# End of layer 0: joining tile 0 by TensorE ahead of a branch, and splitting a weight chunk on ScalarE and VectorE in place of GpSimd

## The chip, the cores and the metric

The kernel runs on one core of one Trainium2 chip. The metric is the device time of one execution in microseconds (us). TensorE is called PE, VectorE DVE, ScalarE ACT, GpSimd POOL and SyncE SP, as in the profile.

## The reference, cut to what matters

A model of two layers works on 256 latent and 256 context tokens of 1024 features. Each layer is a mixer (layer 0: convolution and neighbourhood attention; layer 1: windowed attention), a residual with a layer norm, a mixture of 16 experts of which each token uses two, and a second residual with a layer norm. What matters here is the seam between the layers:

```python
h_lat = layer_norm(alpha * h_lat + m_lat[5] * y[:, y.shape[1] - n_lat:], ln_g[i, 1], ln_b[i, 1])
if need_ctx:
    h_ctx = layer_norm(alpha * h_ctx + m_ctx[5] * y[:, :n_ctx], ln_g[i, 1], ln_b[i, 1])
...
u_lat = h_lat * (1.0 + m_lat[1]) + m_lat[0]
u_ctx = h_ctx * (1.0 + m_ctx[1]) + m_ctx[0]
...
q_lat, k_lat, v_lat = jnp.split(u_lat @ w_in, [q_cols, q_cols + kv_cols], axis=-1)
k_ctx, v_ctx = jnp.split(u_ctx @ w_in[:, q_cols:], [kv_cols], axis=-1)
```

`y` holds for each token the sum of its two experts' rows, each times the token's weight. The layer norm of that sum, turned to feature-major form and scaled, is the input of layer 1's first projections (v, then k, then q).

## The kernel before, in words

The 512 tokens are four tiles of 128 rows, `nt(0)` to `nt(3)` (the SBUF tiles N). In `moe` the experts' work runs in 11 units; each unit's rows are multiplied by the modulation and scattered to a DRAM tensor `yd` with two slots per token. The last two units (`TAIL0 = 2`) are not scattered: their rows stay in SBUF (`self.last`, the tiles wh), and `comb(t, i, p)` brings the rows of unit i to tile t by two TensorE products with a matrix of weights, one for each half of 512 features, into a pair of PSUM banks p.

What the other units gave comes from DRAM: `join_load` reads for tile t both slots, 1024 features each, into one 128x2048 buffer (`zs[t]`; tiles 0 and 1 are named wl, tiles 2 and 3 x). `join_first(t)` adds slot 0 times the token's weight to N, by one DVE instruction (tile 0, L1986) or by two of POOL, a multiplication in place and an addition (tiles 1 to 3, L1983 and L1984). `join_second(t)` adds slot 1 times its weight by one DVE instruction (L1999).

At the end of the last unit's second `down` half come, in the code's order: `comb(0, 0)` into the pair `self.first`; `overflow`, a branch on a number read from SBUF, which every engine reads and takes by itself and which skips a long body where no expert has too many tokens (L1588, L1589); `join_first(0)` on DVE and `join_first(1)` on POOL; and the multiplication of the last rows (L1510).

Then `run` loads the square root's table and lets ACT round the first weight chunk of layer 1 (w1 chunk 5, the v columns) to its high part (L2432). `u1` follows: `comb(0, 1)`, the combinations of tiles 1 and 2, then for tile t: `sums(t)` adds the PSUM pair to N and takes statistics (DVE, L2037, L2038, and a chain of small instructions with a square root on ACT), `norm(t)` normalises on ACT (L2046), `half(t, h)` transposes four blocks by PE (L567), scales them on ACT (L2058; the last on DVE, L2056), rounds them to the high part H (ACT L2064 for tiles 0 and 1, POOL L2062 for 2 and 3) and takes the low part L on DVE (L2066). Tile t's v products (L411 to L413, in `inproj1`) need H and L of both halves. `split1` computes the first chunk's low part on POOL (L2435). The second chunk (the k columns) is split on POOL in two instructions over 2048 columns, high (L388) and low (L391), behind the joins of tiles 2 and 3; its buffer then goes back to the weight stream, and SP issues the next load (L323). The k projection, the first group of the loop in `inproj1`, uses this split chunk.

Every engine takes its instructions in the order of the code; the plan of `moe` (`plan0`) sets the order up to the last unit, and `u1` is written out by hand.

Of the kernel before, what the change touches and what calls it, by code (L numbers as in the profile page):

```python
# [11 lines left out]
F32 = mybir.dt.float32  # L12
# [4 lines left out]
OP = mybir.AluOpType  # L17
# [41 lines left out]
TAIL0 = 2  # L59
# [212 lines left out]
class Kern:  # L272
# [1152 lines left out]
    def moe(self, td, rt, m5base, m5rows, consts):  # L1425

        nc, W, V = self.nc, self.W, self.nc.vector
# [61 lines left out]
        def down(u, f):  # L1489
            w, give = chunks(dw, u, 2)  # L1490
            p = self.mm()
            self.down(p, hT[u], w, f)
            if f:
                give()
            yield
            if u == N - 1:

                end.append(p)
                if f == 0:
                    yield  # L1500
                    return
                self.first = [self.mm() for h in range(2)]
                for i in range(TAIL0 - 1):
                    self.comb(0, i, self.first)
                self.overflow(4, S, td, rt, m5rows)
                self.join_first(0, rt["wt"], False)
                self.join_first(1, rt["wt"], True)
            for f, p in enumerate(end) if u == N - 1 else ((f, p),):
                s = slice(f * 512, f * 512 + 512)
                V.tensor_tensor(ys[u][:, s], p, ys[u][:, s], op=OP.mult)  # L1510
            yield
# [5 lines left out]
        def turn(u):  # L1517
# [9 lines left out]
                                        op0=OP.is_equal, op1=OP.mult)  # L1527
            if u == N - 2:
                self.affine1()
            if u == N - 1:  # L1530
                for k in range(1, 3):
                    self.after[self.end0 - k] = i.ins.name
                self.limit = self.end0
                self.pump()
# [453 lines left out]
    def comb(self, t, i, p):  # L1988

        y, c, _ = list(self.last.values())[i]  # L1990
        for h in range(2):
            self.nc.tensor.matmul(p[h], c[:, t * 128:t * 128 + 128], y[:, h * 512:h * 512 + 512], start=(i == 0),
                                  stop=(i == TAIL0 - 1), skip_group_check=True)
        return p

    def join_second(self, t, wt):

        n, (z, held) = self.nt(t), self.zs.pop(t)
        self.nc.vector.scalar_tensor_tensor(n, z[:, 1024:2048], wt[:, 1, t:t + 1], n, op0=OP.mult, op1=OP.add)  # L1999
        self.release(held)  # L2000


# [23 lines left out]
    def u1(self, wt):  # L2026
# [41 lines left out]

        def comb(t, p):
            ps[t] = p  # L2070
            for i in range(TAIL0):
                self.comb(t, i, p)

        ps = {0: self.comb(0, TAIL0 - 1, self.first)}
        comb(1, [self.mm(), self.mm()])
        comb(2, [self.pv(), self.aux()])
        self.join_second(0, wt)
        norm(0, sums(0))
        self.join_second(1, wt)
        self.split1()  # L2080
        for t in range(2, 4):
            self.join_first(t, wt, True)
        self.wq.append(self.split(pool=True))
        lo = []
        for t in range(4):
            a, b = half(t, 0), half(t, 1)
            next(a)
            if t < 3:
                rs = sums(t + 1)
            next(a)  # L2090
            if t < 3:
                norm(t + 1, rs)
            if t:
                next(lo.pop())
            if t < 2:
                self.join_second(t + 2, wt)
            next(b)
            next(b)
            if t == 0:
                comb(3, [self.mm(), self.mm()])  # L2100
            next(a)
            lo.append(b)
            if t == 3:
                next(b)
            if t:
                yield t - 1
        for *_, held in self.last.values():
# [488 lines left out]
```

## Time and profile before

| what | us |
|---|---|
| median of 3 runs | 795.43 |
| lowest and highest of them | 790.47 and 797.7 |
| the profiled execution | 796.22 |
| its span in the trace | 794.4 |

The trace is of one execution, the profiled one, and its times count from the span's start; 1.8 us of that execution lie around the span. TensorE is busy for 706.9 us (89%), VectorE 470.4 (59%), ScalarE 278.2 (35%), GpSimd 231.4 (29%). A TensorE product of 128x512 in f32 stands as two records in the trace. The timeline view merges like instructions that follow each other (xN), and its start is the time at which the instruction was taken up, so a wait inside the instruction shows as a longer duration.

### The profile page before, as it was taken

Reading aid. Unit: us, or ns where it says so; the run is one execution under the profiler, and the core shown is the slowest. Engines: PE = TensorE matmul, PEld = TensorE weight load, DVE = VectorE, ACT = ScalarE, POOL = GpSimd, SP = SyncE. Lnnn points to the kernel's source line nnn. Section 1 sums busy time; section 2 is a strip of 40 time slices with the busy share of each in tenths; the row PEclk is TensorE's granted clock in tenths of the full one; section 3 lists DMA queues with packets and bytes.
Section 4 is the critical chain, followed back from the end, with each engine's and each line's share of the span. In section 5 each row is a group of like instructions: output and inputs, shape, how many; then the busy total and the mean of one; then the engine's idle time right before and its main releaser. Section 6 shows DMA issues by size and latency. Waiting matters only on the chain. (4 is left out here: it accounts for less than half of the span.)

```text
span 794.4 us, 11446 instructions
## 1 busy us (share of the span) xinstructions
PE 706.9 (89%) x4162; PEld 414.5 (52%) x4162; DVE 470.4 (59%) x1000; ACT 278.2 (35%) x611; POOL 231.4 (29%) x250
## 2 busy tenths in 40 slices
PE   4799999979989987999999787979999986999992
PEld 0477676724567764434433337856556763454430
DVE  0589897747754878622334298397676388532115
ACT  0541212036775254101100145545677533211121
POOL 1200000037631002854000192163377460111111
PEclk9799999979999997999999997999999997999997
DMA  9974665557459368999997931637645493998892
GB/s 360 388 284 170 239 238 201 224 204 265 142 179 336 120 222 305 376 353 350 413 413 314 386 144 54 212 132 277 282 165 188 179 346 138 412 421 320 349 370 86
DMA packets 36252, 209.64 MB, mean 264 GB/s; under 512 B 4439, under 2 KB 4695, under 8 KB 15056
## 3 DMA queue, kind: packets, MB, share of 16 engines
q1 hardware_dynamic: 27888, 183.56, 59.8%
q10 hardware_dynamic: 4816, 13.85, 5.4%
q0 software_dynamic: 3472, 11.31, 4.0%
q8 instruction: 36, 0.59, 0.3%
q14 instruction: 40, 0.33, 0.1%
HBM read 197.92 MB, written 12.06 MB: 264 GB/s over the span
## 5 line engine op out<-in xcount | busy, mean ns | idle before, releaser
L631 DVE SCALAR_TENSOR_TENSOR x<-x,sm,x 128x512 f32<-128x512 f32 x120 | 90.7, 756 | 3.4
L411 PE MATMUL mm<-H,wh 128*128 128x512 f32 (+1 forms) x208 | 78.5, 378 | 2.4 <-ACT H L614 2.4
L412 PE MATMUL mm<-L,wh 128*128 128x512 f32 (+1 forms) x208 | 76.1, 366 | 0.0
L413 PE MATMUL mm<-H,wl 128*128 128x512 f32 (+1 forms) x208 | 75.9, 365 | 0.2 <-DVE wl L391 0.2
L480 PE MATMUL aux<-w,sc 128*32 128x512 f32 x368 | 53.8, 679 | 17.0 <-ACT sc L444 7.6
L391 DVE TENSOR_TENSOR wl<-w,wh 128x512 fp32r<-128x512 f32 (+1 forms) x27 | 39.1, 1486 | 21.2 <-ACT wh L390 21.0
L401 POOL TENSOR_SCALAR wh<-w 128x256 fp32r<-128x256 f32 x32 | 13.3, 417 | 118.0 <-DMA w<-wo 118.0
L411 PEld LDWEIGHTS mm<-H,wh 128*128 128x128 f32 x208 | 40.2, 193 | 14.3 <-issue 3.4
L699 DVE TENSOR_REDUCE mx<-mm 128x1 f32<-128x512 f32 (+1 forms) x64 | 39.3, 615 | 13.5 <-PE mm L786 7.4
L1838 POOL TENSOR_TENSOR yl<-ada,yh 128x512 fp32r<-128x512 f32 x12 | 15.3, 1274 | 102.3 <-ACT yh L1835 102.3
L412 PEld LDWEIGHTS mm<-L,wh 128*128 128x128 f32 x208 | 40.1, 193 | 7.3 <-DVE L L617 0.8
L413 PEld LDWEIGHTS mm<-H,wl 128*128 128x128 f32 x208 | 40.0, 192 | 7.3 <-DVE wl L391 0.8
L723 ACT COPY pT<-tp 128x512 f32<-128x512 f32 (+1 forms) x64 | 33.9, 530 | 25.2 <-PE tp L721 24.9
L411 PE MATMUL mm<-wh,H 128*128 128x512 f32 x104 | 42.4, 408 | 0.0
L412 PE MATMUL mm<-wl,H 128*128 128x512 f32 x104 | 40.7, 391 | 0.0
L1404 PE MATMUL aux<-x,H 128*32 128x512 f32 (+2 forms) x104 | 38.4, 609 | 0.0
L1510 DVE TENSOR_TENSOR y<-mm,y 128x512 f32<-128x512 f32 x18 | 12.3, 690 | 41.8 <-PE mm L1422 41.7
L390 ACT CAST wh<-w 128x512 fp32r<-128x512 f32 (+1 forms) x27 | 29.6, 1139 | 7.0 <-PE mm L413 6.9
L714 POOL TENSOR_SCALAR pexp<-pexp,ss 128x512 f32<-128x512 f32 x32 | 22.4, 700 | 31.7 <-DVE ss L713 23.8
L413 PE MATMUL mm<-wh,L 128*128 128x512 f32 x80 | 31.4, 393 | 0.0
L714 POOL TENSOR_SCALAR x<-x,ss 128x256 f32<-128x256 f32 (+1 forms) x32 | 21.1, 660 | 32.5 <-DVE ss L713 23.1
L1404 PE MATMUL pv<-w,X 128*32 128x512 f32 (+2 forms) x96 | 30.1, 596 | 0.0
(471 smaller groups left out, 1691.6 us busy)
## 6 DMA issues: line engine op xcount, KB each, us to landing
w<-ada_w SPq DMA_DIRECT2D x46, 1024.0 KB, 6.8
x<-exp SPq DMA_DIRECT2D x35, 1024.0 KB, 13.6
w<-exp SPq DMA_DIRECT2D x32, 1024.0 KB, 6.6
w<-w SPq DMA_DIRECT2D x15, 1024.0 KB, 10.4
wh<-exp SPq DMA_DIRECT2D x12, 1024.0 KB, 10.3
wl<-exp SPq DMA_DIRECT2D x12, 1024.0 KB, 9.6
w<-wo SPq DMA_DIRECT2D x8, 1024.0 KB, 9.8
yd<-x ACTq DMA_DIRECT2D x1, 4096.0 KB, 16.8
```

Source lines behind the costliest of these rows:

```text
L390: self.nc.scalar.copy(h[:, s], w[:, s])
L391: (self.nc.gpsimd if pool or low else self.nc.vector).tensor_tensor(l[:, s], w[:, s], h[:, s].bitcast(F32), op=OP.subtract)
L411: t.matmul(out, ah, bh, start=start, stop=False, skip_group_check=onto)
L412: t.matmul(out, ah, bl, start=False, stop=False, skip_group_check=onto)
L413: t.matmul(out, al, bh, start=False, stop=stop, skip_group_check=onto)
L480: nc.tensor.matmul(p[32 * j:32 * j + 32, :], self.sc[:, kt, :], w[:, j * 512:(j + 1) * 512], start=(kt == 0), stop=(kt == 7), skip_group_c ...
L631: nc.vector.scalar_tensor_tensor(acc[:, i], src, w, acc[:, i], op0=OP.mult, op1=OP.add)
L699: nc.vector.reduce_max(mx, p[:, :nk], axis=AX.X, negate=True)
L714: nc.gpsimd.tensor_scalar(P[i][:, :nk], P[i][:, :nk], r[:, 0:1], 0.0, op0=OP.mult, op1=OP.add)
L723: nc.scalar.copy(T[i][:, :nk], t[:, :nk])
L1404: self.nc.tensor.matmul(p[r], x(kt)[:, r], w_j[:, kt % 4 * 512:kt % 4 * 512 + 512], start=(kt == 0), stop=(kt == 7), skip_group_check=True)
L1838: (V if u == N - 1 else nc.gpsimd).tensor_tensor(lo, y, hi.bitcast(F32), op=OP.subtract)
```

## The change

Tile 0 is joined by PE: `join(0)` adds both slots to the PSUM pair `self.first` by four products with diagonal matrices (identity times the tokens' weight), ahead of `comb(0, 0)` and of the branch. The two diagonals are built by two DVE instructions in the `turn` of the last unit but one. `join_first(0)` and `join_second(0)` on DVE go. Tile 1's second slot is joined by two products with a third diagonal (tile `pexp`, one DVE instruction at the start of `u1`), and `join_second(1)`'s instruction goes. Tile 1's first slot stays on POOL, and tiles 2 and 3 stay as they were.

The combination of tile 2 is moved behind the transposes of tile 0, and that of tile 3 behind those of tile 1. The second weight chunk's high part is one ACT instruction over 2048 columns behind `norm(0)`, its low part four DVE instructions over 512 columns each: two in the turn of tile 2, two in that of tile 3. The two POOL instructions go. The chunk's buffer is given back after the last of the four.

```diff
                 self.first = [self.mm() for h in range(2)]
+                self.join(0, self.first)
                 for i in range(TAIL0 - 1):
                     self.comb(0, i, self.first)
                 self.overflow(4, S, td, rt, m5rows)
-                self.join_first(0, rt["wt"], False)
                 self.join_first(1, rt["wt"], True)
...
             if u == N - 2:
                 self.affine1()
+                self.joins = {}
+                self.join_weights(W.tile([128, 2, 128], F32, name="diag"), ((0, 0), (0, 1)), rt["wt"])
...
+    def join_weights(self, d, which, wt):
+
+        for i, (t, k) in enumerate(which):
+            self.nc.vector.tensor_scalar(d[:, i], self.ident, wt[:, k, t:t + 1], None, op0=OP.mult)
+            self.joins.setdefault(t, []).append((k, d[:, i]))
+
+    def join(self, t, p):
+
+        for i, (k, x) in enumerate(self.joins[t]):
+            for h in range(2):
+                o = k * 1024 + h * 512
+                self.nc.tensor.matmul(p[h], x, self.zs[t][0][:, o:o + 512], start=(i == 0), stop=False, skip_group_check=True)
...
         ps = {0: self.comb(0, TAIL0 - 1, self.first)}
+        self.join_weights(W.tile([128, 4, 128], F32, name="pexp", bufs=5), ((1, 1),), wt)
         comb(1, [self.mm(), self.mm()])
-        comb(2, [self.pv(), self.aux()])
         self.join_second(0, wt)
         norm(0, sums(0))
-        self.join_second(1, wt)
+        w, whole = self.take(), self.held
+        wlo, whi = self.part("wh"), self.part("wl")
+        nc.scalar.copy(whi, w)
         self.split1()
         for t in range(2, 4):
             self.join_first(t, wt, True)
-        self.wq.append(self.split(pool=True))
+        self.wq.append((whi, wlo))
...
-            if t < 2:
-                self.join_second(t + 2, wt)
             next(b)
             next(b)
             if t == 0:
+                comb(2, [self.pv(), self.aux()])
+                self.join_second(1, wt)
+            if t == 1:
                 comb(3, [self.mm(), self.mm()])
+            if t < 2:
+                self.join_second(t + 2, wt)
             next(a)
             lo.append(b)
             if t == 3:
                 next(b)
+            if t > 1:
+                for i in (2 * t - 4, 2 * t - 3):
+                    q = slice(i * 512, i * 512 + 512)
+                    nc.vector.tensor_tensor(wlo[:, q], w[:, q], whi[:, q].bitcast(F32), op=OP.subtract)
+                if t == 3:
+                    self.release(whole)
```

`join_second` keeps only the giving back of the buffer for a tile that is in `self.joins`, and `comb` starts a PSUM pair only where no join has started it.

VectorE behind the branch, before: N is the residual's tile, the wl tiles are the loaded slots, the wh tile of L1510 is the last unit's rows, mm the PSUM pair.

```order
L1986 SCALAR_TENSOR_TENSOR N_1818<-wl_3483,rwt,N_1818 128x1024
L1510 TENSOR_TENSOR wh_3438<-mm,wh_3438 128x512 x2
L1999 SCALAR_TENSOR_TENSOR N_1818<-wl_3483,rwt,N_1818 128x1024
L2037 TENSOR_TENSOR N_1818<-N_1818,mm 128x512
L2038 BN_STATS bst<-N_1818 128x6
```

VectorE at the same place, now:

```order
L1510 TENSOR_TENSOR wh_3441<-mm,wh_3441 128x512 x2
L2001 TENSOR_SCALAR pexp<-cb,rwt 128x128
L2053 TENSOR_TENSOR N_1818<-N_1818,mm 128x512
L2054 BN_STATS bst<-N_1818 128x6
L2053 TENSOR_TENSOR N_1818<-N_1818,mm 128x512
L2054 BN_STATS bst<-N_1818 128x6
```

Both joins of tile 0 are gone from VectorE, and one diagonal has come in.

GpSimd behind the branch, before: the second tile wl and the tiles x are the loaded slots, w of L2435 is the first chunk's low part, wh and the wl of L391 the second chunk's parts, H the high part of the transposed tiles.

```order
L1983 TENSOR_SCALAR wl_3487<-wl_3487,rwt 128x1024
L1984 TENSOR_TENSOR N_1818<-N_1818,wl_3487 128x1024
L2435 TENSOR_TENSOR w_6110<-x_3490,x_6109 128x2048
L1983 TENSOR_SCALAR x_3492<-x_3492,rwt 128x1024
L1984 TENSOR_TENSOR N_1819<-N_1819,x_3492 128x1024
L1983 TENSOR_SCALAR x_3495<-x_3495,rwt 128x1024
L1984 TENSOR_TENSOR N_1819<-N_1819,x_3495 128x1024
L388 TENSOR_SCALAR wh_6162<-w_3498 128x2048
L391 TENSOR_TENSOR wl_6163<-w_3498,wh_6162 128x2048
L2062 TENSOR_SCALAR H_6120<-pT 128x4x128
```

GpSimd at the same place, now:

```order
L2464 TENSOR_TENSOR w_6116<-x_3493,x_6115 128x2048
L1985 TENSOR_SCALAR x_3495<-x_3495,rwt 128x1024
L1986 TENSOR_TENSOR N_1819<-N_1819,x_3495 128x1024
L1985 TENSOR_SCALAR x_3498<-x_3498,rwt 128x1024
L1986 TENSOR_TENSOR N_1819<-N_1819,x_3498 128x1024
L2078 TENSOR_SCALAR H_6126<-pT 128x4x128
```

The two instructions over the second chunk are gone, and the rounding of tile 2 follows the joins directly.

TensorE from the branch to the transposes of tile 1, before: the wh tiles are the rows of the last two units, cb holds the identity, mm, pv and aux are PSUM banks.

```order
L1992 MATMUL mm<-wh_3438 128x512 x2
L1992 MATMUL mm<-wh_3348 128x512 x2
L1992 MATMUL mm<-wh_3438 128x512 x2
L1992 MATMUL pv<-wh_3348 128x512
L1992 MATMUL aux<-wh_3348 128x512
L1992 MATMUL pv<-wh_3438 128x512
L1992 MATMUL aux<-wh_3438 128x512
L567 MATMUL tp<-cb,N_1818 128x128 x8
```

TensorE at the same place, now:

```order
L1994 MATMUL mm<-wh_3441 128x512 x2
L2009 MATMUL mm<-wl_3490,pexp 128x512 x2
L1994 MATMUL mm<-wh_3348 128x512 x2
L1994 MATMUL mm<-wh_3441 128x512 x2
L567 MATMUL tp<-cb,N_1818 128x128 x8
L1994 MATMUL pv<-wh_3348 128x512
L1994 MATMUL aux<-wh_3348 128x512
L1994 MATMUL pv<-wh_3441 128x512
L1994 MATMUL aux<-wh_3441 128x512
```

Two products for tile 1's second slot have come in, and the combination of tile 2 stands behind the transposes of tile 0.

## Rows read from the trace of the kernel before

**Rows 1.** The page: the span.

```profile
span 794.4 us, 11446 instructions
```

**Rows 2.** The table by stretch, late layer 1: us, busy per engine, PEclk, DMA share, GB/s.

```profile
680.00:700.00 20.00, 19.95 (x99) 11.00 (x100) 10.54 (x21) 3.66 (x9) 2.55 (x2) 1.00 1.01 422
```

**Rows 3.** Timeline of DVE, 453 to 493: start, duration, line, operation, idle before and releaser.

```profile
453.20 3.29 DVE L1986 SCALAR_TENSOR_TENSOR N<-wl,rwt,N 128x1024 f32<-128x1024 f32 x1 [4.83 <-DVEq L1589]
456.42 1.27 DVE L1510 TENSOR_TENSOR wh<-mm,wh 128x512 f32<-128x512 f32 x2
457.62 5.58 DVE L1999 SCALAR_TENSOR_TENSOR N<-wl,rwt,N 128x1024 f32<-128x1024 f32 x1
463.30 0.69 DVE L2037 TENSOR_TENSOR N<-N,mm 128x512 f32<-128x512 f32 x1
...
474.28 5.00 DVE L2066 TENSOR_TENSOR L<-pT,H 128x512 fp32r<-128x512 f32 x1
479.20 0.67 DVE L2037 TENSOR_TENSOR N<-N,pv 128x512 f32<-128x512 f32 x1
...
492.58 0.69 DVE L2066 TENSOR_TENSOR L<-pT,H 128x512 fp32r<-128x512 f32 x1 [2.15 <-POOL H L2062]
```

**Rows 4.** Timeline of POOL, 448 to 479.

```profile
448.51 1.12 POOL L1983 TENSOR_SCALAR wl<-wl,rwt 128x1024 f32<-128x1024 f32 x1 [13.73 <-DMA wl<-yd]
453.07 2.34 POOL L1984 TENSOR_TENSOR N<-N,wl 128x1024 f32<-128x1024 f32 x1 [3.44 <-DVEq L1589]
457.62 4.50 POOL L2435 TENSOR_TENSOR w<-x,x 128x2048 fp32r<-128x2048 f32 x1 [2.21 <-ACT x L2432]
462.10 2.08 POOL L1983 TENSOR_SCALAR x<-x,rwt 128x1024 f32<-128x1024 f32 x1
...
466.59 1.12 POOL L1983 TENSOR_SCALAR x<-x,rwt 128x1024 f32<-128x1024 f32 x1
467.80 3.20 POOL L1984 TENSOR_TENSOR N<-N,x 128x1024 f32<-128x1024 f32 x1
...
473.37 5.36 POOL L391 TENSOR_TENSOR wl<-w,wh 128x2048 fp32r<-128x2048 f32 x1
```

**Rows 5.** Timeline of ACT: the first chunk's rounding and the first norm.

```profile
455.66 1.88 ACT L2432 CAST x<-x 128x2048 fp32r<-128x2048 f32 x1
...
467.19 1.24 ACT L2046 ACTIVATE N<-N,brs 128x1024 f32<-128x1024 f32 x1 [0.48 <-DVE brs L550]
```

**Rows 6.** Timeline of PE: combinations, and first and last of the k projection.

```profile
451.77 1.98 PE L1992 MATMUL mm<-wh 128*128 128x512 f32 x4
457.15 6.81 PE L1992 MATMUL mm<-wh 128*128 128x512 f32 x12 [3.39 <-DVE wh L1510]
...
497.84 0.39 PE L411 MATMUL mm<-H,wh 128*128 128x512 f32 x1
...
509.12 1.07 PE L480 MATMUL aux<-w,sc 128*32 128x512 f32 x8
```

**Rows 7.** The branch's line on PE: duration min/median/max in ns, first and last start.

```profile
L1589 PEldq COMPARE_BRANCH  x1: 5837/5837/5837, 448.9 to 448.9; - x1
```

**Rows 8.** The table by stretch, 473 to 498, columns as in rows 2.

```profile
473.00:477.00 4.00, 1.57 (x11) 1.12 (x10) 4.00 (x2) 3.97 (x10) 3.92 (x2) 1.00 0.00 0
477.00:486.00 9.00, 5.24 (x23) 4.95 (x24) 8.56 (x13) 4.04 (x10) 1.73 (x1) 0.50 0.35 118
...
489.00:498.00 9.00, 8.30 (x70) 7.87 (x69) 4.69 (x10) 4.67 (x11) 2.53 (x4) 1.00 0.00 0
```

**Rows 9.** Timeline of SP and of ACT: a weight load's issue, and its chunk's split.

```profile
478.76 0.33 SPq L323 DMA_DIRECT2D w<-w  x1
...
514.62 2.18 ACT L390 CAST wh<-w 128x512 fp32r<-128x512 f32 x4
```

**Rows 10.** Timeline of DVE: idle behind a turn's one-hot tiles, and such tiles.

```profile
420.69 0.69 DVE L1510 TENSOR_TENSOR y<-mm,y 128x512 f32<-128x512 f32 x1 [1.21 <-PE mm L1422]
...
433.59 2.14 DVE L1526 TENSOR_SCALAR rgb<-cb,rrk,wlast 128x128 f32<-128x128 f32 x8
```

More of the change, by code (lines that the diff above doesn't have):

```diff
@@ L1991, in comb @@
         for h in range(2):
-            self.nc.tensor.matmul(p[h], c[:, t * 128:t * 128 + 128], y[:, h * 512:h * 512 + 512], start=(i == 0),
-                                  stop=(i == TAIL0 - 1), skip_group_check=True)
-        return p
+            self.nc.tensor.matmul(p[h], c[:, t * 128:t * 128 + 128], y[:, h * 512:h * 512 + 512],
+                                  start=(i == 0 and t not in self.joins), stop=(i == TAIL0 - 1), skip_group_check=True)
+        return p
+    def join_weights(self, d, which, wt):
[7 more added lines that the diff above has]
+                self.nc.tensor.matmul(p[h], x, self.zs[t][0][:, o:o + 512], start=(i == 0), stop=False, skip_group_check=True)
     def join_second(self, t, wt):
         n, (z, held) = self.nt(t), self.zs.pop(t)
-        self.nc.vector.scalar_tensor_tensor(n, z[:, 1024:2048], wt[:, 1, t:t + 1], n, op0=OP.mult, op1=OP.add)
+        if t not in self.joins:
+            self.nc.vector.scalar_tensor_tensor(n, z[:, 1024:2048], wt[:, 1, t:t + 1], n, op0=OP.mult, op1=OP.add)
         self.release(held)
@@ L2070, in comb @@
             ps[t] = p
+            if t in self.joins:
+                self.join(t, p)
             for i in range(TAIL0):
```

## The prediction

> **What bounds the kernel now.** I read the page first, for the span of 794.4 us [rows 1], then the table by stretch for the part behind the seam, and then, between 448 and 510 us, the timeline of one engine after the other, since the change touches nothing else. In that stretch TensorE waits for others, and the reader should follow who. DVE comes out of the branch at 453.2 and joins tile 0 in 3.29 us, multiplies the last rows in 1.27, joins tile 0's second slot in 5.58, and only at 463.30 begins `sums(0)` [rows 3]. PE had stood idle 3.39 us for DVE's last rows [rows 6].
>
> The long durations have one cause that can be read by laying DVE's rows over POOL's. DVE's join of 453.20 ends at 456.49; POOL's addition of 453.07 had ended at 455.41, 1.08 us before. DVE's join of 457.62 ends at 463.20; POOL's subtraction of 457.62 had ended at 462.12, 1.08 us before. DVE's low part of 474.28 ends at 479.28; POOL's of 473.37 ended at 478.73, 0.55 before [rows 3, 4]. So a DVE instruction that reads two SBUF tensors starts its work when POOL's running instruction is over, and takes 1.08 us (1024 columns) or 0.55 (512). It holds in the other direction too: POOL's multiplication of 462.10 takes 2.08 us, that of 466.59 takes 1.12 [rows 4], and the difference of 0.96 is what was left of DVE's join. A DVE instruction that reads PSUM and one SBUF tensor isn't held: 0.69 us at 463.30 beside POOL's 462.10 [rows 3, 4].
>
> So the seam's end is set by this chain: POOL's joins end at 471.00, then POOL splits the second chunk until 478.73, DVE's low part of tile 0 sits behind that, `sums(2)` starts at 479.20, and norm, transposes and v products of tiles 2 and 3 follow until the k projection starts at 497.84 [rows 3, 4, 6].
>
> **The change part by part.** *Diagonals.* Three DVE instructions of 128x128, 2.14/8 = 0.27 us each [rows 10]. Two stand in the turn behind which DVE idles 1.21 us [rows 10]: 0.54 of it, hidden. The third stands behind L1510.
>
> *PE ahead of the branch.* Two combination products took 1.98 us with their drain, so 0.99 each at most [rows 6]. Four joins and `comb(0, 0)` are 6 x 0.99 = 5.9, from 451.8 to 457.7. Their operand is there: POOL took up tile 1's slot, loaded later than tile 0's, at 448.51 [rows 4]; were it late, `comb(0, 0)` and the branch would be queued behind the wait. PE's branch starts at 448.9 and lasts 5.84, to 454.7 [rows 7], so it lies beside these products as long as PE's sequencer still runs ahead of them.
>
> *DVE behind the branch.* Two joins go, 3.29 + 5.58 = 8.87 us [rows 3]. L1510 ends at 453.2 + 1.27 = 454.5, the diagonal at 454.8, both before PE is done at 457.7. What is late next is PE: the first half of `comb(0, 1)` ends at 458.7, `sums(0)` starts at 458.8 instead of 463.30, and the first norm, 3.89 us behind it as before (463.30 to 467.19) [rows 3, 5], at 462.7: 4.5 us earlier.
>
> *Tile 1.* PE goes on with the second half (459.7), two joins (461.7) and the combination (465.6, its first half done at 464.7). `sums(1)` starts there and DVE is free 3.9 us later, at 468.6. With products of 0.86 instead of 0.99 it would be 466.9.
>
> *POOL.* The first chunk's low part hangs on ACT's rounding, which hangs on the branch alone; so POOL again starts tile 2's join at 462.10, and now no DVE instruction with two SBUF inputs stands in its way: 1.12 + 2.34 + 1.12 + 2.34 with 0.1 between them [rows 4] end at 469.2 instead of 471.00. The two instructions over the second chunk, until 478.73, are gone.
>
> *The turn of tile 2.* DVE asks for tile 2's second join between 466.9 and 468.6. That lies inside POOL's last addition (466.9 to 469.2), so the join is held until 469.2 and ends at 470.3; tile 0's low part takes 0.6 more, and `sums(2)` starts at 470.9 instead of 479.20. This is the term: 8.3 us. It is the same for any request of DVE in that interval, so neither PE's price nor the diagonal's decides it. The combination of tile 2, moved behind the eight transposes, must be there: 465.6 + 1.1 + 4 x 0.99 = 470.7, its first half 1 us earlier. Just in time. The bounds: at 0.86 us DVE asks 1.7 us earlier, and if it slips in ahead of POOL's addition, that addition holds tile 0's low part instead, so at best another 0.5 us; if PE is 2 us later than thought, 2 us are lost.
>
> *High part on ACT.* One cast of 2048 columns, 1.88 us [rows 5], from 464 to 466 behind `norm(0)`. It delays ACT's scaling of tile 0's first half by under 2 us, which nothing waits for before DVE's low part at 470.3. Costed at nothing; without that cover it is 1.88. The cast also waits for the chunk's load, which is issued ahead of the branch and of which no row here gives the landing; behind the cast are queued the scaling of tile 0 and the second norm, so a landing later than 466 would cost its lateness.
>
> *Low part on DVE.* Four instructions of 512 columns with two SBUF inputs, 0.69 each, as the one of 492.58 [rows 3]. Two stand ahead of tile 2's second low part, where DVE idled 2.15 us waiting for POOL [rows 3]: 1.4 us, hidden. Two stand behind the last low part, while PE still has the v products of tiles 2 and 3; the k projection's first columns need none of them. If one met POOL's rounding it would wait some 0.6 us, still inside the idle time.
>
> *The buffer of the second chunk* comes back after the last quarter, some 489, instead of 478.76; the next load is issued then. ACT splits that chunk at 514.62 [rows 9], in the changed kernel at 506; 17 us are left for one transfer of 1 MB. At 422 GB/s, as in [rows 2], it takes 2.5.
>
> **The sum.** -8.3 us at `sums(2)`; the path from there to the k projection, 479.20 to 497.84, is the same work. Behind it PE stays nearly saturated (19.95 of 20 us in [rows 2]). 796.22 - 8.3 = 787.9 for an execution like the profiled one. That one lay 0.8 above the median of 795.43, so the forecast is 787.1.
>
> **The rivals.**
> [...]
>
> [...]
>
> *The branch on PE.* If PE reads the flag only when its products are done (457.7), the branch ends at 457.7 + 0.6 + 5.8 = 464.1 and everything on PE is 6.4 later; DVE's request moves from 468.6 to 475.0, and of the 8.3 some 2.4 us are left: 793.0. Against: before, the branch started at 448.9, ahead of products that began at 451.77 [rows 6, 7].
>
> *Hidden anyway.* If layer 1's expert loads, at a DMA share of 1.01 [rows 2], set the end and don't move with the seam, part of the gain is lost; half of it gives 791.2. Against: their issue waits for buffers and a routing that PE's work sets.
>
> **How the numbers follow.** Forecast 0.66, half clock in the products 0.12, branch 0.06, hidden anyway 0.08, slower 0.08. Two of the runs before lie 7 us apart, so the forecast's own range is 787.1 with 4 to each side; the cases at 791 and part of that at 793 belong to the eight tenths: 783.0 to 793.5. A measurement of this kernel tells about 1% from no change, here 787.5; the forecast lies just past it. Of its 0.66 I put 0.44 beyond the line and 0.22 within; the three smaller gains go to within, with 0.02 of them beyond; that makes 0.46 faster, 0.46 within, 0.08 slower.
>
> **What would show it.** Right: no DVE instruction over 3.5 us between 453 and 490; `sums(0)` near 458.5, the first norm near 462.5; POOL's joins over at 469; `sums(2)` near 471; the k projection's first product near 489.5. Wrong: a branch on PE that ends after 458; combinations of tile 2 later than 471, so that DVE waits for PE; a granted clock of 0.50 between 477 and 500; ACT waiting for the delayed chunk near 506; or a distance from the k projection's start to the span's end other than 296.6 us (794.4 - 497.84).

## The result, and the profile after

The changed kernel takes 789.23 us (median of 20 runs, 786.9 to 790.88) against 795.44 us for the kernel before in the same session (20 runs, 790.47 to 797.7). The ratio is 0.9931, with a 95% interval of 0.9917 to 0.9946: 5.5 us faster, 4.3 to 6.6. That is inside the forecast range of 783.0 to 793.5, 2.1 us above the forecast of 787.1, and a gain of less than 1%. The profiled execution took 789.16 us, with a span of 787.4 against 794.4 [rows 1].

The timeline of the changed kernel from the branch to the k projection, as the prediction went through it. First DVE. L2053 is `sums`, L2015 `join_second`, L2082 a low part of H, L2131 the quarters of the second chunk's low part; the columns are those of rows 3.

```profile
453.60 1.29 DVE L1510 TENSOR_TENSOR wh<-mm,wh 128x512 f32<-128x512 f32 x2 [5.50 <-DVEq L1591]
457.11 0.29 DVE L2001 TENSOR_SCALAR pexp<-cb,rwt 128x128 f32<-128x128 f32 x1 [2.22 <-issue]
458.36 0.69 DVE L2053 TENSOR_TENSOR N<-N,mm 128x512 f32<-128x512 f32 x1 [0.96 <-PE mm L1994]
...
463.58 0.69 DVE L2053 TENSOR_TENSOR N<-N,mm 128x512 f32<-128x512 f32 x1 [1.37 <-POOL w L2464]
...
467.33 1.92 DVE L2015 SCALAR_TENSOR_TENSOR N<-x,rwt,N 128x1024 f32<-128x1024 f32 x1
469.18 2.84 DVE L2082 TENSOR_TENSOR L<-pT,H 128x512 fp32r<-128x512 f32 x1
471.94 0.67 DVE L2053 TENSOR_TENSOR N<-N,pv 128x512 f32<-128x512 f32 x1
...
483.04 1.28 DVE L2131 TENSOR_TENSOR wh<-w,wl 128x512 fp32r<-128x512 f32 x2
```

The joins of 3.29 and 5.58 us [rows 3] are gone; no DVE instruction between 453 and 490 lasts longer than 2.84. `sums(0)` starts at 458.36 instead of 463.30, `sums(2)` at 471.94 instead of 479.20. The quarters cost DVE 0.64 each and nobody waits for them.

POOL, whose chain sets `sums(2)`:

```profile
459.03 4.52 POOL L2464 TENSOR_TENSOR w<-x,x 128x2048 fp32r<-128x2048 f32 x1 [3.21 <-DMA w<-w]
463.53 1.12 POOL L1985 TENSOR_SCALAR x<-x,rwt 128x1024 f32<-128x1024 f32 x1
464.74 2.35 POOL L1986 TENSOR_TENSOR N<-N,x 128x1024 f32<-128x1024 f32 x1
467.07 1.11 POOL L1985 TENSOR_SCALAR x<-x,rwt 128x1024 f32<-128x1024 f32 x1
468.27 3.20 POOL L1986 TENSOR_TENSOR N<-N,x 128x1024 f32<-128x1024 f32 x1
```

The row of 459.03 puts POOL's wait down to a load, but ACT's rounding, whose result it subtracts, had ended only 0.08 before (458.95), and in the eight executions that have this order POOL starts 1.97 to 1.98 behind the rounding's start. Tile 2's join starts 1.43 us later than in [rows 4] (463.53 against 462.10). The reason stands in ACT's timeline and in the branch's line on PE, whose columns are those of rows 7:

```profile
457.05 1.90 ACT L2461 CAST x<-x 128x2048 fp32r<-128x2048 f32 x1 [1.58 <-PEq L1591]
462.24 1.24 ACT L2062 ACTIVATE N<-N,brs 128x1024 f32<-128x1024 f32 x1 [0.48 <-DVE brs L550]
463.39 1.90 ACT L2099 CAST wl<-w 128x2048 fp32r<-128x2048 f32 x1
```

```profile
L1591 PEldq EVENT_SEMAPHORE  x2: 51/51/51, 457.0 to 457.1; - x2
L1591 PEldq COMPARE_BRANCH  x1: 6079/6079/6079, 450.3 to 450.3; - x1
```

The same semaphores in the kernel before:

```profile
L1589 PEldq EVENT_SEMAPHORE  x2: 51/51/51, 454.8 to 455.0; - x2
```

ACT's rounding of the first chunk now waits 1.58 us, and what releases it is a semaphore that PE sets behind its branch (at 457.0). The branch itself is over earlier, at 450.3 + 6.08 = 456.4; the last of the six products that stand ahead of it on PE ends at 455.04 + 1.88 = 456.92. So the semaphore comes when the products are through, not when the branch is. Before, the branch was over at 448.9 + 5.84 = 454.7 [rows 7], the semaphore came at 454.8, and the rounding followed ACT's own table load without a wait [rows 5]. The second chunk's rounding (463.39) costs nothing, as forecast.

PE itself, with the columns of rows 6:

```profile
447.92 3.65 PE L1422 MATMUL mm<-w,hT 128*64 128x512 f32 x16 [0.52 <-ACT hT L1412]
451.51 3.70 PE L2009 MATMUL mm<-wl,diag 128*128 128x512 f32 x8
455.04 1.88 PE L1994 MATMUL mm<-wh 128*128 128x512 f32 x4
457.22 1.96 PE L1994 MATMUL mm<-wh 128*128 128x512 f32 x4 [0.30 <-PEq L1591]
...
490.58 0.39 PE L411 MATMUL mm<-H,wl 128*128 128x512 f32 x1
```

The idle 3.39 us at the branch [rows 6] has become 0.30, and the k projection starts at 490.58 instead of 497.84. Of the 7.3 us between the two, 0.3 is the earlier start of the first row.

**A measure for the experiments.** Single executions differ by several us ahead of the change: the sixteen products with which the half pass ends (L1422, the first row above) started anywhere from 445.3 to 451.2. So I use the seam: from that start to the first product of the k projection. Behind it the rest of the span is 295.9 to 297.3 us in thirteen executions and 299.3 in one. All numbers below are us behind the seam's start; the runs are explained in the next section.

| execution | `sums(0)` | `sums(2)` | from there to the k projection | seam |
|---|---|---|---|---|
| before, first | 15.11 | 31.01 | 18.64 | 49.65 |
| before, second | 10.79 | 26.41 | 19.46 | 45.87 |
| after, first | 10.44 | 24.02 | 18.64 | 42.66 |
| after, second | 10.44 | 24.02 | 20.05 | 44.07 |
| after, third | 10.44 | 24.03 | 18.85 | 42.88 |
| after, fourth | 10.50 | 24.04 | 20.04 | 44.08 |
| split alone | 14.87 | 26.01 | 18.66 | 44.67 |
| join alone | 10.43 | 24.02 | 21.23 | 45.25 |
| join behind the branch | 16.18 | 26.95 | 19.17 | 46.12 |
| cast ahead | 11.76 | 22.31 | 19.38 | 41.69 |
| cast and diagonal ahead | 10.44 | 21.22 | 19.38 | 40.60 |
| diagonal ahead | 10.43 | 24.03 | 20.05 | 44.08 |
| old order | 10.43 | 24.31 | 18.86 | 43.17 |
| low part between | 10.43 | 24.03 | 22.09 | 46.12 |

### The profile page after: what moved, and what is told of

It reads as the page before. It is cut to its first block, busy times and chain, and to the rows that moved or that the text cites. A ratio compares the mean times of both kernels' runs of the same rounds, so it can differ in the third digit from the quotient of the medians.

```text
span 787.4 us, 11473 instructions
## 1 busy us (share of the span) xinstructions
PE 710.8 (90%) x4174; PEld 415.4 (53%) x4174; DVE 460.8 (59%) x1004; ACT 280.2 (36%) x612; POOL 223.8 (28%) x248
## 5 line engine op out<-in xcount | busy, mean ns | idle before, releaser
L411 PE MATMUL mm<-H,wh 128*128 128x512 f32 (+1 forms) x192 | 72.9, 380 | 1.6 <-ACT H L614 1.6
L412 PE MATMUL mm<-L,wh 128*128 128x512 f32 (+1 forms) x192 | 70.5, 367 | 0.0
L413 PE MATMUL mm<-H,wl 128*128 128x512 f32 (+1 forms) x192 | 70.3, 366 | 0.0
L391 DVE TENSOR_TENSOR wl<-w,wh 128x512 fp32r<-128x512 f32 (+1 forms) x27 | 39.0, 1481 | 19.9 <-ACT wh L390 19.7
L411 PEld LDWEIGHTS mm<-H,wh 128*128 128x128 f32 x192 | 37.9, 197 | 13.0 <-issue 3.4
L412 PEld LDWEIGHTS mm<-L,wh 128*128 128x128 f32 x192 | 37.8, 197 | 6.3 <-DVE L L617 0.4
L413 PEld LDWEIGHTS mm<-H,wl 128*128 128x128 f32 x192 | 37.7, 196 | 6.1 <-DVE wl L391 0.2
L1510 DVE TENSOR_TENSOR y<-mm,y 128x512 f32<-128x512 f32 x18 | 12.3, 690 | 41.2 <-PE mm L1422 41.1
```

The source lines that it names most:

```text
L391: (self.nc.gpsimd if pool or low else self.nc.vector).tensor_tensor(l[:, s], w[:, s], h[:, s].bitcast(F32), op=OP.subtract)
L411: t.matmul(out, ah, bh, start=start, stop=False, skip_group_check=onto)
L412: t.matmul(out, ah, bl, start=False, stop=False, skip_group_check=onto)
L413: t.matmul(out, al, bh, start=False, stop=stop, skip_group_check=onto)
```

## The experiments

The theory at the start: DVE and POOL hold each other; the change takes their meetings away, 8.3 us by forecast, and PE's later passing of the branch, which ACT's rounding waits for, gives 1 to 1.5 back. The rivals: one part alone does all; the gain is PE's, from its order or its clock.

**The split alone.** The kernel before with the second chunk's high part on ACT and its low part on DVE; the join of tile 0 as before.

```
-        self.wq.append(self.split(pool=True))
+        w, whole = self.take(), self.held
+        wlo, whi = self.part("wh"), self.part("wl")
+        nc.scalar.copy(whi, w)
...
+        self.wq.append((whi, wlo))
...
```

> The kernel before with only the second chunk's split changed (high part on ACT behind the first norm, low part on DVE in quarters); the joins stay on DVE. Theory 'lock' (the gain comes from POOL's 7.3 us over the chunk no longer holding DVE's low part): DVE asks for tile 2's second join near 472.6, POOL is done at 471.0, so sums(2) starts near 474.4 instead of 479.2, and the time falls by about 4.8 us. Rival 'joins' (the gain comes from the 8.9 us of DVE joins ahead of the first norm): the first norm stays at 467, and the time falls by less than 1 us.

Measured: 791.24 us (788.91 to 793.79), ratio 0.9946 (0.9924 to 0.9968) to the 795.98 of that session. `sums(2)` comes 5.00 earlier than in the first execution of before, and the seam is 4.98 shorter, as the theory 'lock' expected (4.8). Tile 0's joins still last 3.30 and 4.99 us.

**The join alone.** The changed kernel with the second chunk's split on POOL again, behind tile 3's combination.

```
...
-        nc.scalar.copy(whi, w)
...
                 comb(3, [self.mm(), self.mm()])
+                wlo, whi = self.part("wh"), self.part("wl")
+                self.wq.append(self.split(pool=True, bufs=(whi, wlo)))
...
```

> The changed kernel with the second chunk's split given back to POOL (two instructions over 2048 columns, behind the combination of tile 3). Theory 'lock': sums(2) still starts near 472, but POOL's low part then runs from about 474 to 478.6 and holds DVE's low part of tile 0's second half until 479, so sums(3) is some 3 us later than in the changed kernel and only 4 us of the gain over the kernel before remain. Rival 'joins': all of the gain remains, within 1 us of the changed kernel.

Measured: 791.22 us (789.95 to 793.8), ratio 0.9943 (0.9923 to 0.9962); the seam is 4.40 shorter. POOL's long subtraction meets a low part of DVE again, that of tile 0's second half:

```profile
473.34 4.55 POOL L391 TENSOR_TENSOR wh<-w,wl 128x2048 fp32r<-128x2048 f32 x1
```

```profile
475.17 3.27 DVE L2082 TENSOR_TENSOR L<-pT,H 128x512 fp32r<-128x512 f32 x1
478.36 1.27 DVE L2015 SCALAR_TENSOR_TENSOR N<-x,rwt,N 128x1024 f32<-128x1024 f32 x1
```

POOL's instruction ends at 477.89, DVE's 0.55 later, the number of [rows 3, 4]. So each part alone is worth 4.4 to 5.0 us of the seam and both together 7.0 against the first execution of before. Against its second execution (below) the parts are worth 1.2 and 0.6 and both together 3.2, so the seams of single executions don't carry this alone. The times of all runs do: by their ratios the split is worth 4.3 us (2.5 to 6.0), the join 4.5 (3.0 to 6.1) and both together 5.5 (4.3 to 6.6), less than the sum of the parts. Both hang on one chain through POOL, and their gains overlap.

**The join behind the branch.** The changed kernel with the six products moved behind the call of the branch.

```
+                self.overflow(4, S, td, rt, m5rows)
                 self.join(0, self.first)
                 for i in range(TAIL0 - 1):
                     self.comb(0, i, self.first)
-                self.overflow(4, S, td, rt, m5rows)
```

> The changed kernel with tile 0's four join products and comb(0, 0) behind the branch instead of ahead of it. Theory 'PE's branch' (the changed kernel lost about 1 us because the products ahead of the branch delay PE's branch by 1.4 us, and ACT's rounding of the first chunk, and POOL behind it, wait for PE's branch): the rounding starts near 455.7 again and POOL's joins end 1.4 us earlier, but PE's products come 2 to 3 us later, so sums(0) moves from 458.4 to about 460.5 and sums(2) stays within 0.5 us of the changed kernel. If PE's granted clock falls to half in the idle time at the branch, 2 to 3 us slower than the changed kernel. Rival 'the products ahead are hidden, nothing waits for PE's branch': the rounding does not move, and the kernel is 2 us slower.

Measured: 790.49 us (789.71 to 791.31), ratio 0.9932 (0.9912 to 0.9953). PE's clock, from the table by stretch (columns as in rows 2):

```profile
450.00:452.00 2.00, 0.00 (x0) 0.00 (x0) 1.29 (x2) 0.37 (x1) 1.72 (x1) 0.82 0.97 387
452.00:454.00 2.00, 1.66 (x2) 0.84 (x3) 0.00 (x0) 1.99 (x3) 0.62 (x1) 0.50 1.03 414
```

```profile
452.34 6.54 PE L2009 MATMUL mm<-wl,diag 128*128 128x512 f32 x8 [3.37 <-PEq L1591]
```

```profile
L1591 PEldq COMPARE_BRANCH  x1: 5897/5897/5897, 446.0 to 446.0; - x1
```

```profile
458.98 0.60 DVE L2001 TENSOR_SCALAR pexp<-cb,rwt 128x128 f32<-128x128 f32 x1 [7.29 <-issue]
```

PE idles 3.37 us in the branch, the granted clock falls to 0.50, and eight join products take 6.54 us instead of 3.70. `sums(0)` comes 5.74 later and the seam is 3.46 longer than after's first; the median time is 1.3 us higher, and the ratio to the kernel before is that of the changed kernel (0.9932 and 0.9931). So the seam of this one execution doesn't stand for the kernel's time, and why it grew by more stays open. At the same time PE goes into the branch 0.7 us behind the seam's start (446.0), as before, not 2.4 (450.3); it is through at 451.9, with none of the six products ahead of it, and ACT's rounding starts without a wait, 7.72 behind the seam's start instead of 9.13. POOL's joins are over 2.3 us earlier (21.3 behind the seam's start, not 23.6) and hold nobody in the turn of tile 2. So the products ahead of the branch have a price (what PE sets behind the branch waits for them) and a return the prediction had not counted: with them in that place the clock did not fall here. In the kernel before the clock fell at this place too, behind the 3.39 us of [rows 6]:

```profile
458.00:460.00 2.00, 2.00 (x4) 0.81 (x3) 2.00 (x1) 0.00 (x0) 2.00 (x1) 0.50 1.00 401
```

In all four executions of the changed kernel it stayed at 1.00 from the seam's start to beyond `sums(2)`.

**The cast ahead.** The changed kernel with ACT's rounding of the first chunk ahead of the branch, so that it need not wait for what PE sets behind it.

```
+                w, held = self.take(), self.held
+                b = [self.borrow(F32R, False) for _ in range(2)]
+                nc.scalar.copy(b[0][0], w)
+                self.first1 = w, held, b
                 self.overflow(4, S, td, rt, m5rows)
...
```

> The changed kernel with ACT's rounding of the first chunk moved ahead of the branch, so that neither it nor POOL's low part behind it waits for PE's branch. Theory 'PE's branch': the rounding runs near 449 to 451, POOL's low part starts right behind tile 1's join near 456 instead of 459.0, POOL's joins are over near 467.5 instead of 471.5, tile 2's second join is not held, sums(2) starts near 469.2 instead of 471.9, and the time falls by a further 2.5 us. Rival 'the seam is bound elsewhere' (PE's combinations, or a wait for a load): less than 0.5 us.

Measured: 788.26 us (786.68 to 789.33), ratio 0.9900 (0.9879 to 0.9921); `sums(2)` 1.71 earlier than after, the seam 0.97 shorter than after's first, less than the 2.5 expected. Three rows of its timeline say why:

```profile
453.72 1.90 ACT L1508 CAST x<-x 128x2048 fp32r<-128x2048 f32 x1 [4.67 <-DMA x<-yd]
```

```profile
459.56 1.39 DVE L2005 TENSOR_SCALAR pexp<-cb,rwt 128x128 f32<-128x128 f32 x1 [4.11 <-ACTq L1595]
```

```profile
456.36 4.51 POOL L2466 TENSOR_TENSOR w<-x,x 128x2048 fp32r<-128x2048 f32 x1
```

The rounding waited for a transfer, so ACT came out of the branch itself 4.5 us later (its table load started 10.56 behind the seam's start, not 6.05); DVE's third diagonal waits for that (`ACTq`), and then POOL's subtraction, until 460.87, held it: 1.39 us instead of 0.29. `sums(0)` came 1.3 late.

**The diagonal ahead, and cast and diagonal ahead.** The third diagonal goes to unused columns of the buffer that the last turn borrows, ahead of the branch: once alone, once with the cast.

```
+                self.join_weights(b[:, 1536:1664].rearrange("p (i n) -> p i n", i=1), ((1, 1),), rt["wt"])
...
-        self.join_weights(W.tile([128, 4, 128], F32, name="pexp", bufs=5), ((1, 1),), wt)
```

> The changed kernel with DVE's third diagonal alone ahead of the branch; ACT's rounding stays behind it. Theory 'ACT's rounding carries PE's delay to POOL': the seam stays 42.7 within 0.4 us, POOL's joins end 23.5 us behind the seam's start, sums(2) 24.0. Rival 'the diagonal behind the branch carries it': sums(0), 10.4 behind the start, comes 1 us earlier, and the seam shrinks by 1 us or more.

> The changed kernel with both things that wait for PE's passing of the branch put ahead of it: ACT's rounding of the first chunk of layer 1's weights (as in the run with the rounding alone ahead), and DVE's third diagonal, which goes to unused columns of the buffer that the last turn borrows. Theory 'passing of the branch': ACT's later passing no longer reaches DVE, so sums(0) starts 10.4 us behind the seam's start (the last sixteen products of the half pass), as in the changed kernel, not 11.8; POOL's joins are over 18.9 behind it; the product of tile 2's second half is not held by POOL; sums(2) starts 21.3 behind it (24.0 in the changed kernel, 22.3 with the rounding alone ahead), the seam is 40.1 long against 42.7, and the time about 2.5 us under the changed kernel's. Rival 'two diagonals and the PE set sums(0) anyhow': sums(0) stays at 11.8 and the seam within 0.5 us of 41.7. Rival 'the next engine takes over' (ACT, which passes its branch 1.3 us later and loads its table behind it, or PE): sums(2) comes as above, the seam shrinks by less than 1.5 us against the changed kernel's 42.7.

Alone (one execution, 791.05 us): `sums(0)` 10.43 and `sums(2)` 24.03, nothing moved, so it is not the diagonal that carries PE's delay. The seam is 44.08; the clock fell behind `sums(2)`, to 0.50 from 481.90 to 483.90, as in two executions of the changed kernel (below). With the cast: 786.66 us (786.05 to 790.44), ratio 0.9901 (0.9868 to 0.9935) to 795.27; the changed kernel beside it on the same chip took 788.98, ratio 0.9928 (0.9899 to 0.9957). `sums(2)` comes at 21.22 against the 21.3 expected:

```profile
467.69 2.37 POOL L1991 TENSOR_TENSOR N<-N,x 128x1024 f32<-128x1024 f32 x1
```

```profile
470.57 1.28 DVE L2020 SCALAR_TENSOR_TENSOR N<-x,rwt,N 128x1024 f32<-128x1024 f32 x1
471.77 0.69 DVE L2087 TENSOR_TENSOR L<-pT,H 128x512 fp32r<-128x512 f32 x1
472.37 0.68 DVE L2058 TENSOR_TENSOR N<-N,pv 128x512 f32<-128x512 f32 x1
```

POOL is done at 470.06, before DVE asks: 1.28 and 0.69 instead of 1.92 and 2.84. This is the seam without any hold, 40.60 long, 2.06 to 3.48 under after's four; the theory's 40.1 was missed by 0.5, since from `sums(2)` on it took 19.38 and not 18.64, at the full clock (1.00 in every 2 us): all of tile 3's combination (3.60 us of products, begun at 473.93) now lies behind `sums(2)`, in the changed kernel 2.35 of it (470.69 to 474.29, with `sums(2)` at 471.94). By time the intervals of the two ratios overlap, and the medians lie 2.3 us apart; by median it is the fastest of the kernels here. So POOL's late chain, with its holds, costs the changed kernel 2.8 us at `sums(2)`. That is more than the wait for PE's semaphore: the cast ahead of the branch takes away that wait (1.58 us) and with it ACT's own way through the branch and its table load, and POOL's subtraction starts 7.32 behind the seam's start instead of 11.11.

**The old order.** The changed kernel with the combinations of tiles 2 and 3 in the places of before. The release of tile 1's buffer, which the expectation names too, stayed in the loop.

```
+        comb(2, [self.pv(), self.aux()])
         self.join_second(0, wt)
...
             if t == 0:
-                comb(2, [self.pv(), self.aux()])
                 self.join_second(1, wt)
-            if t == 1:
                 comb(3, [self.mm(), self.mm()])
```

> The changed kernel with the combinations of tiles 2 and 3 and the release of tile 1's buffer in the places of the kernel before; the join of tile 0 by PE and the split of the second chunk stay as changed. Theory 'POOL's joins set sums(2)': POOL's chain does not depend on these places, DVE's product of tile 2's second half and the low part are held until POOL's last addition as before, sums(2) starts 24.0 us behind the seam's start, and the seam is 42.7 long, at most 0.5 us either way. Rival 'PE has to be kept free ahead of the transposes': the seam is 1.5 us longer or more, as tile 2's combination (3.8 us of products) stands ahead of tile 0's transposes again.

Measured: 789.33 us (787.13 to 791.53), ratio 0.9931 (0.9909 to 0.9954); the seam 43.17, inside after's 42.66 to 44.08. These moves are worth nothing that can be measured here.

**Both kernels once more.** No edit.

> The kernel before once more, for its seam in a second profiled execution. If the seam before is as steady as its first part, it is 49.65 us within 0.4, with sums(2) 31.0 behind its start and 18.64 from sums(2) to the k projection, at the same half clock in the first 8 us behind sums(2). Rival: the clock decides there too, and with another clock the seam comes out 1 us or more shorter or longer.

> The changed kernel itself once more, beside the others on the same chip, for its seam in a second profiled execution and its time. Expected: 5.5 us under the kernel before (4.3 to 6.6), the seam 42.7 us within 0.4, of which the stretch up to sums(2) is 24.0; the stretch from the first product of the k projection to the end 296.8. If the seam should be 1 us or more away from 42.7, the lengths of single profiled executions can't carry differences of that size.

> The changed kernel, a third profiled execution. Its first had the full clock from sums(2) to the k projection, and 18.64 us there; its second fell to half clock (0.50) for about 3 us from 12 us behind sums(2), behind PE's wait of 1.8 us for the low part of tile 1's second half, and had 20.05. Theory 'the clock falls behind that wait in some executions': the stretch is again one of these two lengths (18.6 or 20.0, within 0.2), the shorter one where the granted clock stays at 1.00, the longer where it falls, and sums(2) comes 24.02 behind the seam's start in both cases. Rival 'something else moves it': another length, or the longer one at the full clock.

> The changed kernel, a fourth profiled execution; the same expectations as for the third.

The kernel before, second execution (792.95 us), came out with a seam of 45.87 instead of 49.65. So the seam before is not steady, as the rival said, but not through the clock, as it supposed. The rows that answer to the 457.62 of [rows 3] and of [rows 4], and PE's branch, in this second execution:

```profile
457.54 1.27 DVE L1999 SCALAR_TENSOR_TENSOR N<-wl,rwt,N 128x1024 f32<-128x1024 f32 x1
```

```profile
458.48 4.71 POOL L2435 TENSOR_TENSOR w<-x,x 128x2048 fp32r<-128x2048 f32 x1 [3.14 <-ACT x L2432]
```

```profile
456.50 1.90 ACT L2432 CAST x<-x 128x2048 fp32r<-128x2048 f32 x1 [1.22 <-PEq L1589]
```

```profile
L1589 PEldq COMPARE_BRANCH  x1: 7399/7399/7399, 449.0 to 449.0; - x1
```

The same branch took PE 7.40 us, not the 5.84 of [rows 7]. ACT's rounding waited 1.22 us for it, POOL's subtraction slipped from 457.62 to 458.48, and DVE's join, ready at 457.54, went first: 1.27 us instead of 5.58, `sums(0)` 4.3 earlier. In the profiled execution both had started at 457.62, a tie that POOL won; in the split alone POOL was 0.6 ahead (455.58 to 456.17) and won too. What carries the gain on to `sums(2)` is a second meeting, since POOL's joins were over no earlier than before (471.22, to 471.00 in [rows 4]):

```profile
471.31 2.75 POOL L388 TENSOR_SCALAR wh<-w 128x2048 fp32r<-128x2048 f32 x1
```

```profile
472.23 2.37 DVE L2066 TENSOR_TENSOR L<-pT,H 128x512 fp32r<-128x512 f32 x1
```

DVE, ahead of its first time by 2 us, asked for the low part of tile 0 while POOL still rounded the second chunk, and had it 0.54 behind that rounding's end (474.06 to 474.60), ahead of the long subtraction; in the first execution it asked at 474.28, behind the subtraction's start, and had to wait for its end at 478.73 [rows 3, 4]. The kernel before has two ways to go there; the changed one has neither DVE's joins of tile 0 nor POOL's two instructions at the place, and its `sums(2)` comes at 24.02 to 24.04 in all four executions.

The changed kernel's second, third and fourth executions (792.48, 790.96 and 789.59 us) give 20.05, 18.85 and 20.04 from `sums(2)` to the k projection. Two of four are 1.2 to 1.4 longer, so by what was said ahead of the second execution the seams of single executions can't carry differences of this size, the 0.97 of the cast ahead among them. The stretch up to `sums(2)`, steady to 0.02 us in the four, can. The table by stretch at that place, first execution, then second:

```profile
481.94:483.94 2.00, 1.37 (x12) 1.37 (x13) 2.00 (x4) 1.99 (x4) 0.00 (x0) 1.00 0.00 0
483.94:485.94 2.00, 1.77 (x17) 1.54 (x16) 1.00 (x3) 2.00 (x7) 0.62 (x1) 1.00 0.00 0
```

```profile
483.72:485.72 2.00, 1.36 (x10) 1.36 (x10) 2.00 (x4) 1.98 (x4) 0.00 (x0) 0.90 0.00 0
485.72:487.72 2.00, 2.00 (x11) 2.00 (x11) 1.00 (x2) 1.63 (x6) 0.62 (x1) 0.50 0.00 0
```

In both, PE has just waited for a low part of DVE, 1.83 us in the first and 1.84 in the second; in the second the granted clock then fell to 0.50 (eleven products in 2 us, not seventeen), in the first it stayed at 1.00. Long seams and a fallen clock go together in all four: from 8 to 16 us behind `sums(2)` the clock was 1.00, 0.79, 1.00 and 0.79.

**The low part between.** The changed kernel with the low part that PE waits 1.83 us for put between the two halves of `sums(3)`.

```
-        def sums(t):
+        def sums(t, mid=None):
...
+                if mid and h == 0:
+                    next(mid)
...
```

> The changed kernel with one instruction of DVE moved: the low part of tile 1's second half of H stands between the two halves of sums(3) and no longer behind the norm, so PE's wait of 1.83 us for it (its 8 x 3 products of the first output chunk) goes, and the second half of sums(3), with what hangs on it, comes 0.6 us later. Theory 'the clock falls behind that wait in some executions': the granted clock stays at 1.00 from sums(2) to the k projection, and the stretch is 18.6 to 19.3 us; the median time is 0 to 1 us under the changed kernel's. Rival 'the wait does not matter': the clock falls there all the same, or the stretch is 20 us or more; the median time is that of the changed kernel or up to 0.6 us over it.

Measured: 790.86 us (788.37 to 792.36), ratio 0.9938 (0.9916 to 0.9960) to 795.58, 1.6 us above the changed kernel's median. The theory's forecast fell: the stretch took 22.09 and the clock fell for longer. The rival had the stretch right (20 or more) and the time too low (up to 0.6 above).

```profile
482.48 0.76 PE L567 MATMUL tp<-cb,N 128*128 128x128 f32 x4 [1.98 <-ACT N L2064]
```

```profile
484.00:486.00 2.00, 2.00 (x10) 2.00 (x11) 1.45 (x4) 1.48 (x5) 0.95 (x2) 0.50 0.00 0
486.00:488.00 2.00, 2.00 (x12) 2.00 (x11) 1.49 (x4) 0.00 (x0) 1.17 (x2) 0.50 0.00 0
```

The wait did not go, it moved: PE did its products earlier and then idled 1.98 us for the norm of tile 3, and the half clock now fell on the gapless v products behind it. What decides in which executions of one kernel the clock falls behind such a wait stays open.

## Why the prediction was right, and where it was off

**Right.** DVE without long instructions, `sums(0)` (458.36, forecast 458.5) and the first norm (462.24 against 462.5), the high part on ACT and the low part on DVE at no cost, a span behind the k projection's start that does not move (296.8 against 296.6), and the third chunk, whose load now goes out at 490.37 and which ACT splits at 507.37 without a wait. The path from `sums(2)` to the k projection, "the same work" in the prediction, was right by luck: it took 18.64 us in both profiled executions, but before its first 8 us ran at half clock (0.50) [rows 8] with no combination in it, and after it ran at full clock (1.00) with 2.35 us of tile 3's. The hold itself works as read: POOL's last addition took 3.20 us because DVE's join ran ahead of it, and DVE's low part of 469.18 ended 0.55 us behind that addition (471.47 to 472.02).

**The step that failed: POOL.** The prediction said that the first chunk's low part hangs on ACT's rounding, "which hangs on the branch alone", so that tile 2's join would start at 462.10 again and POOL's joins be over at 469.2. The rounding hangs on the later of two things: ACT's own way out of the branch, and a semaphore that PE sets behind its branch. In rows 5 the first was later, and the second could not be seen. PE sets it when both the branch and the products queued ahead of the branch are through. Before, that was the branch (454.7, with `comb(0, 0)` over earlier); the four join products that the change queues ahead of it (step "PE ahead of the branch") made it the products (456.92, the branch 456.4). In all eight executions with the six products ahead of the branch and the rounding behind it, the rounding starts 9.13 us behind the seam's start, while the branch took PE from 5.90 to 6.12: the branch's length doesn't reach it. So the second became the later, and the joins were over at 471.47: 1.43 from the start, 0.85 from the last addition, held by DVE's join that now slipped in ahead of it. Of that, `sums(2)` keeps 1.3: it comes 24.02 behind the seam's start, where the term of 8.3 puts it at 31.01 - 8.3 = 22.7. Three runs show the cause: without products ahead of the branch the rounding doesn't wait (the join behind the branch, 7.72); with a longer branch on PE it waits in the kernel before too (1.22 us, second execution); and with the rounding ahead of the branch POOL holds nobody and `sums(2)` comes at 21.22.

**The rival of the clock came true in part.** The prediction gave half clock in the products a chance of 0.12 and, as its author's estimate, a price of 4 us; a case at 791 in its range stands for it. No run shows a price of that size. What the four executions of the changed kernel show is a fallen clock in two, over some 3 us, at a cost of 1.2 to 1.4: 0.76 us on the mean of the four seams over the shortest. Together 1.3 + 0.76 = 2.1, about the distance of 789.2 from 787.1. That the two agree so closely is luck in part: single executions differ by several us ahead of the seam, and the kernel before has two seams.

**The profiled execution was taken for the kernel.** The 5.58 us join was one outcome of a tie, and a longer branch on PE undoes it. The mean of after's four seams is 43.42: 6.2 under the first execution of before, 2.5 under the second. That the ratio of all runs gives 5.5, less than the 6.2, is what a mixture of the two would do: with the second kind in a share s of the runs, 6.2 - 3.8 s = 5.5 gives s of about 0.2. This is an estimate, and a loose one: the ratio's interval of 4.3 to 6.6 allows any share from 0 to 0.5, and the share itself was not measured. The prediction took 0.8 us off for an execution above the median, where the two equal start times asked for a second case.

**The other rivals.** The branch on PE began at 450.3, ahead of the join products (451.51), not behind them, so that rival fell in the form it had. What it feared for the branch happened to the semaphore behind the branch, which did wait for the products: that is the step above. Nothing was hidden behind layer 1's loads, and the k projection ran at full clock (1.00 over the 11.28 us from 490.58 to 501.86), so the slower case, with its 0.08, fell too.

**Loose details** that don't move the sum: what was left of DVE's join beside POOL's 462.10 was 1.10 us by [rows 3, 4], not 0.96, and POOL's four instructions add up to 469.3, not 469.2.

## What to carry to other kernels

When work is put ahead of a branch on one engine, look for everything on the other engines that is released by what that engine sets behind it: here that came only when the work ahead was through. Such a wait can be invisible before, because something else comes last. Two instructions that become ready at the same time and hold each other are a race: the kernel before has one in its chain, and its two executions have `sums(2)` at 31.01 and 26.41 us; without it the changed kernel has 24.02 to 24.04 in four. Compare a stretch between two fixed instructions, in more than one execution, before a difference of 1 us is believed.

## What the runs showed of the hardware that had not been expected

- Passing the branch, whose body is skipped, took PE 5.84 us and 7.40 us in two executions of the same kernel [rows 7, and the row above].
- A DVE instruction with one SBUF input can be held by POOL too: the 128x128 multiplication took 0.29 us without POOL's subtraction beside it, and 1.39 (cast ahead) and 0.60 (join behind the branch) with it, and in both ended 0.08 us behind the subtraction (460.95 to 460.87, 459.58 to 459.50). The statistics, which also read one SBUF tensor, were not held: 0.69 at 464.30 in the changed kernel, beside POOL's multiplication of 463.53, and 0.69 at 465.61, beside its addition of 464.74. Why the multiplication is held and the statistics are not, no row here shows.
- Behind the same wait, of 1.83 to 1.84 us, the granted clock fell in two executions of the changed kernel (0.79 from 8 to 16 us behind `sums(2)`, as low as 0.50 in the second execution) and stayed at 1.00 in two.
